# A two-layer attention trunk on one core: the first stage put in another order

## The chip, the cores and the metric

The kernel runs on one core of a Trainium2 chip. The metric is device time in microseconds (us) of one execution; three runs are given, and a profiled execution beside them. The engines: TensorE (PE, matrix products into PSUM), VectorE (DVE), ScalarE (ACT), GpSimd (POOL), and SyncE (SP), which issues most transfers.

## The reference

One sequence of 512 tokens, width 1024, two layers, each `x + rmsnorm(mixer(rmsnorm(x)))`. Layer 0 mixes by sparse attention with three branches (compressed, selected, window) in 16 heads and 4 groups, layer 1 by differential attention in 8 heads:

```python
for i in range(DEPTH):                       # 2
    u = rmsnorm(x, norm_pre[i])
    y = nsa_mixer(u, ...) if i % 2 == 0 else diff_mixer(u, ...)
    x = x + rmsnorm(y, norm_post[i])
# nsa_mixer
q, kc, vc, ks, vs, kw, vw, gate, z = split(u @ w_in)     # 1024 x 3632
o = gate0 * o_c + gate1 * o_s + gate2 * o_w              # gate = sigmoid
y = (o * silu(z)) @ w_out
# diff_mixer
q, k, v, z = split(u @ w_in)                             # 1024 x 4096
a = softmax(q1 k1 + bias) - lam * softmax(q2 k2 + bias)
y = (rmsnorm(a @ v) * (1 - lambda_init) * silu(z)) @ w_out
```

With 512 tokens all 8 selection blocks are taken, so that the selected branch is dense and causal, and the window of 512 covers the sequence.

## The kernel before

**Precision.** A projection splits each operand into a high and a low fp32r part and sums three products (high-high, low-high, high-low), line 197. Weight tiles stream from HBM: `Stream.load` (line 114) issues a transfer on SP, `Stream.split` (line 131) makes the two parts, for most tiles both on POOL (lines 165, 167); for the first two tiles the table `SP0`, `SP1` says by quarter which engine makes which (A: ACT, D: DVE, P: POOL). Each split loads the tile after next (line 170).

**Jobs.** All projections are a list of jobs, in the order in which the weights stream. `mjob` (line 190) makes 128 output columns for all tokens, 24 matmuls of 512 columns; `tjob` (line 205) makes token-major outputs, by weight tile or, with `by_token`, token by token. Each job is a generator and has a cost in ns: 5,120 for an mjob, and for a tjob by `4 * KD * 3 * n / 2.4` (line 242) with n columns: 10,240 for `vs` (n = 256), 12,160 for `vw` (n = 304). The job list begins `vs`, `vw`, then `kc0`, `kc1`, `vc0` and so on; index 2 is the first after the two.

**The pacing.** `Runner` (line 244) pulls jobs between other work. `step` runs one piece of the current job and adds its ns to the count; `upto` runs until a job is over; `spread` shares what is left up to a job among a number of slots; `knots` sets goals by head from the summed costs; `pull`, called after every score slot, runs pieces until the count is at the goal or the job limit is reached:

```python
self.done += next(self.gen)                                              # step, 255
total = sum(j.cost for j in jobs[:self.limit]) - self.done               # spread, 268
self.base, self.per = self.done, total / max(nslots, 1)                  # 269
self.ks = [(0, self.done)] + [(k, sum(j.cost for j in jobs[:index[n] + 1])) for k, n in ks]   # knots, 274
while self.i < self.limit and self.done < self.goal():                   # pull, 284
    self.step()
```

**The first stage.** SP issues the first token block (128 tokens), the two row broadcasts of the pre-norm gain (line 298, one row of 1024 values read into all 128 partitions), two weight tiles and then the other three token blocks (lines 608 to 612). `prenorm` (line 355) normalises a block: ACT squares and sums it, DVE scales it by the row's factor and the gain, PE transposes it (line 380), ACT copies the high part (`hi`, L100), DVE subtracts for the low part (`lo`, L105). Lines 665 to 668 do this for the four blocks, with 8 `run.step()` after each, and a scheduler orders the engines' work by priority. The PSUM banks are named by their use: `S` and `mm` two each, `T` three, `av` one.

**The first mixer's attention.** After the key projections and the compression (109.7 us), four groups follow (line 968). A group has eight units, `qb` in the order 3, 0, 2, 1 and both branches each, and a unit has four score slots: two score matmuls (lines 800, 801), the soft maximum (lines 792, 794), a scaling (line 850), transposes (line 856), products with V (line 870). A ninth unit, `Cmp` (its DVE product of line 918), ends the group. For groups 0 to 2 line 977 spreads four mjobs over 33 slots: `run.spread(ends[g], 33)`; before the next group `run.upto` finishes what is left. Group 3 spreads two jobs and the output projection's first part. The first half of a group is slots 1 to 16 (`qb` 3 and 0), the second half slots 17 to 32.

**The second mixer.** The second pre-norm and the value projections `dv0` to `dv3` come at about 350 to 432 us (line 1089 on; there too two jobs run as generators, and line 1100 adds their cost to the count). Then eight heads of four units with two score slots each (line 1198 on); line 1197 sets the goals of the heads' jobs, `run.upto(dends[h])` ends each head, and after the heads the output projection follows.

## Time and profile before

| | |
|---|---|
| median of 3 runs | 672.92 us (671.29 to 674.07) |
| the profiled execution | 666.73 us |
| its span, first to last instruction | 664.8 us |
| PE busy | 638.5 us (96%) |
| DVE, ACT, POOL busy | 434.2, 340.6, 402.5 us |
| first value matmul, first key projection | 11.27, 43.27 us |
| groups 0 to 3 begin | 109.7, 164.83, 220.02, 274.11 us |
| their second halves begin | 135.17, 189.46, 244.94, 293.00 us |
| the eight heads | 432 to 612 us |

PE's matmuls are pipelined: a record lasts longer than the distance from one start to the next, so a cost is read from starts, and a busy PE may still have room. "Granted clock" is the share of full speed that PE's clock had; 0.50 is 1.2 GHz, 1.00 is 2.4 GHz.

### The profile page before, as it was taken

What the parts mean: (1) busy time and instruction counts of PE and PEld (TensorE: products, weight loads), DVE (VectorE), ACT (ScalarE), POOL (GpSimd) and SP (SyncE); (2) the same over time, 40 slices, a digit from 0 to 9 for tenths busy, and PEclk for the clock granted to TensorE, in tenths of its full rate; (3) what the DMA queues carried; (4) which work ended last, traced back from release to release, by engine and by line L of the source; (5) the groups of instructions that cost most, each with busy time, mean ns of one, the idle gap of its engine ahead of it and who ended that gap; (6) DMA issues with size and microseconds to landing.
All of it is one profiled execution on the core that took longest, in us unless ns stands there. A gap on an engine that the chain in (4) does not pass through costs nothing.

```text
span 664.8 us, 11267 instructions
## 1 busy us (share of the span) xinstructions
PE 638.5 (96%) x3773; PEld 555.4 (84%) x3773; DVE 434.2 (65%) x1224; ACT 340.6 (51%) x904; POOL 402.5 (61%) x675
## 2 busy tenths in 40 slices
PE   6999999999999999999999899999999999899996
PEld 5888888888788788888887899888888887779885
DVE  4611235688878878969878700147859769996834
ACT  5311234675667567778553311235455556577531
POOL 4778568777778587758487358948465464332300
PEclk8999999999999999999999899999999999999998
DMA  7565433113022121201942222323223222114402
GB/s 251 141 166 134 124 80 93 53 34 84 12 65 65 33 63 29 53 17 48 322 149 93 96 64 76 116 65 110 65 76 84 72 72 65 64 63 155 164 26 101
DMA packets 68989, 60.52 MB, mean 91 GB/s; under 512 B 3628, under 2 KB 60868, under 8 KB 68932
## 3 DMA queue, kind: packets, MB, share of 16 engines
q1 hardware_dynamic: 68212, 57.45, 29.6%
q10 hardware_dynamic: 720, 2.36, 0.9%
q8 instruction: 30, 0.49, 0.3%
q14 instruction: 27, 0.22, 0.1%
HBM read 55.04 MB, written 4.76 MB: 90 GB/s over the span
## 4 chain that ended last, share of the span: by engine, by line
PE 74%; DVE 15%; ACT 5%; issue 3%; DMA 2%; POOL 0%; SPq 0%; DVEq 0%; ACTq 0%; POOLq 0%
PE mm L198 28%; PE mm L218 10%; PE mm L467 6%; PE T L856 5%; PE av L870 5%; PE S L218 5%; PE S L801 4%; PE S L800 3%; PE S L467 3%; DVE stk L105 3%; DVE P L792 1%; PE T L721 1%; PE av L1162 1%; DMA wraw<-in_nsa_w_in_dram 1%; ACT stk L100 1%
## 5 line engine op out<-in xcount | busy, mean ns | idle before, releaser
L167 POOL TENSOR_TENSOR wlo<-wraw,whi 128x256 fp32r<-128x256 f32 (+2 forms) x247 | 185.5, 779 | 22.9 <-DVE st L792 12.1
L165 POOL TENSOR_SCALAR whi<-wraw 128x256 fp32r<-128x256 f32 (+1 forms) x240 | 95.6, 424 | 115.0 <-PE mm L198 54.9
L794 ACT ACTIVATE P<-P,st 128x512 f32<-128x512 f32 (+3 forms) x192 | 107.4, 560 | 89.2 <-DVE st L792 88.3
L850 POOL TENSOR_SCALAR P<-P,st,gate 128x512 f32<-128x512 f32 (+3 forms) x128 | 80.1, 639 | 27.3 <-DVE st L847 22.6
L198 PE MATMUL mm<-bigA,whi 128*128 128x512 f32 x192 | 77.3, 403 | 0.1
L792 DVE CUSTOM_DVE_ANT_0 P<-S,BT 128x128 f32<-128x128 f32 (+2 forms) x144 | 59.7, 418 | 24.2 <-PE S L801 21.9
L198 PE MATMUL mm<-bigB,whi 128*128 128x512 f32 x192 | 75.4, 393 | 0.0
L198 PE MATMUL mm<-bigA,wlo 128*128 128x512 f32 x192 | 75.3, 392 | 0.0
L105 DVE TENSOR_TENSOR PT<-T,PT 128x512 fp32r<-128x512 f32 x84 | 56.9, 685 | 8.2 <-ACT PT L100 6.2
L870 PE MATMUL av<-PT,bigE 128*128 128x512 f32 x160 | 56.4, 417 | 1.1 <-DVE bigF L878 0.9
L100 ACT ACTIVATE stk<-mm 64x512 fp32r<-64x512 f32 x64 | 37.9, 591 | 33.2 <-PE mm L198 17.8
L218 PE MATMUL mm<-whi,bigF 128*128 128x256 f32 x176 | 50.4, 288 | 2.3 <-DVE stk L105 2.3
L856 PE MATMUL T<-ident,P 128*128 128x128 f32 x320 | 51.7, 272 | 0.0
L100 ACT ACTIVATE PT<-T 128x512 fp32r<-128x512 f32 x84 | 48.6, 591 | 6.1 <-PE T L856 3.9
L856 PEld LDWEIGHTS T<-ident,P 128*128 128x128 f32 x320 | 41.0, 140 | 12.3 <-issue 0.4
L198 PE MATMUL mm<-bigF,whi 128*128 128x512 f32 x128 | 51.1, 399 | 0.0
L421 DVE SCALAR_TENSOR_TENSOR stk<-mm,stk 64x512 fp32r<-64x512 f32 x32 | 22.1, 690 | 44.5 <-ACT stk L100 43.7
L198 PE MATMUL mm<-bigF,wlo 128*128 128x512 f32 x128 | 50.5, 395 | 0.0
L198 PE MATMUL mm<-bigE,whi 128*128 128x512 f32 x128 | 50.2, 392 | 0.0
L218 PE MATMUL mm<-wlo,bigF 128*128 128x256 f32 x176 | 49.9, 284 | 0.0
L218 PE MATMUL mm<-whi,bigE 128*128 128x256 f32 x176 | 49.4, 283 | 0.0
L198 PEld LDWEIGHTS mm<-bigB,whi 128*128 128x128 f32 x192 | 36.0, 188 | 8.1
(286 smaller groups left out, 1675.3 us busy)
## 6 DMA issues: line engine op xcount, KB each, us to landing
wraw<-in_diff_w_in_dram SPq DMA_DIRECT2D x31, 512.0 KB, 3.8
wraw<-in_nsa_w_in_dram SPq DMA_DIRECT2D x26, 512.0 KB, 4.0
BT<-rd SPq DMA_DIRECT2D x32, 128.0 KB, 3.2
wraw<-in_diff_w_out_dram SPq DMA_DIRECT2D x5, 512.0 KB, 3.8
bigF<-in_x_dram SPq DMA_DIRECT2D x4, 512.0 KB, 9.8
wraw<-in_nsa_w_out_dram SPq DMA_DIRECT2D x4, 512.0 KB, 3.5
bigD<-in_x_dram SPq DMA_DIRECT2D x4, 512.0 KB, 4.2
x1d<-bigD ACTq DMA_DIRECT2D x4, 512.0 KB, 5.1
```

Source lines behind the costliest of these rows:

```text
L100: return nc.scalar.activation(dst, src, AF.Copy, scale=scale)
L105: nc.vector.tensor_tensor(dst, src, h.bitcast(F32), op=OP.subtract)
L165: nc.gpsimd.tensor_scalar(h[:, a:b], v, 1.0, 0.0, op0=OP.mult, op1=OP.add)
L167: e.tensor_tensor(l[:, a:b], v, h[:, a:b].bitcast(F32), op=OP.subtract)
L198: T["mm"] = nc.tensor.matmul(p[:, a:b], wt[:, k, :], u[:, k, a:b], start=(k == 0 and j == 0), stop=(k == KD - 1 and j == 2)).ins
L218: nc.tensor.matmul(acc[t], u[:, k0 + k, t * 128:(t + 1) * 128], wt[:, k, :], start=(ci == 0 and k == 0 and j == 0 and t % per == 0), stop= ...
L467: nc.tensor.matmul(p, U[u][:, k, t * 128:(t + 1) * 128], wt[wi], start=start and j == 0, stop=stop and j == 2, skip_group_check=True)
L792: nc.vector.tensor_tensor_reduce(out=o, in0=i0, in1=b, op0=OP.add, op1=OP.min, scale=-1.0, scalar=BIG, accum_out=nm)
L794: nc.scalar.activation(pt[:, :n], pt[:, :n], AF.Exp, bias=nm, scale=-1.0, accum_out=den)
L850: NORM(nc, i, br, qb).tensor_scalar(self.P[i][:, :n], self.P[i][:, :n], st[:, 8 + i:9 + i], gate[:, NT - 1 - qb, c:c + 1], op0=OP.mult, op ...
L856: T["tmark"] = nc.tensor.transpose(p[:, j * 128:(j + 1) * 128], self.P[j][:, kb * 128:(kb + 1) * 128], ident).ins
L870: nc.tensor.matmul(av, T["V"][:, br, kb, g, :], p, start=(br == 0 and kb == 0 and j == 0), stop=(br == 1 and kb == qb and j == 1))
```

## The change

The gain row is no longer broadcast by transfers. One row goes by ACT's queue into the first partition of a zeroed tile, and two fp32 matmuls with a matrix of ones write it to all partitions of two PSUM banks. The first token block comes in two half transfers, the second one is issued ahead of the weights. The first five weight tiles are split by a table with high parts on ACT and low parts on DVE and POOL. The order of PE in the first stage is written out in `SEQ0` (s, w: one token of `vs`, `vw`; p: the transposes of a token block), `vw` goes token by token too, and the two generators are called directly; afterwards `run.i` is set to 2. The tanh of the gate is taken once at the end. `nsplit` says how many tiles a `by_token` job splits when it ends. A `by_token` job now takes one bank for each token.

```diff
-WARM = 7
+WARM = 4
...
-NS = 4
+NS = 5
...
+SEQ0 = 's0 p1 s1 w0 w1 p2 s2 w2 p3 w3 s3'.split()
-SPX = ('AP',) * 4
-SPN = 2
-SP0 = ('AP',)*4
-SP1 = ('AD','AD','PP','PP')
+SP0 = (('AP', 'AD', 'AP', 'AP'), ('AD', 'AP', 'AD', 'AP'), ('AP', 'AP', 'AD'), ('AP', 'AP', 'AD'), ('AP', 'AD'))
...
             evac(p)
         Job(name, [wcols(w, width, col, 128)], run, 24 * 512 / 2.4)
 
-    def tjob(name, w, width, col, n, evac, banks, cuts=((0, 4), (4, 4)), by_token=False):
+    def tjob(name, w, width, col, n, evac, banks, cuts=((0, 4), (4, 4)), by_token=False, nsplit=None):
         def run(i):
-            bs = [bank(b) for b in banks]
-            per = 4 // len(bs)
-            acc = [bs[t // per][:, (t % per) * n:(t % per) * n + n] for t in range(NT)]
+            if by_token:
+                per, acc = 1, [None] * NT
+            else:
+                bs = [bank(b) for b in banks]
+                per = 4 // len(bs)
+                acc = [bs[t // per][:, (t % per) * n:(t % per) * n + n] for t in range(NT)]
             cut = {}
 
             def part(ci, t):
...
                     yield 3 * n / 2.4
 
             if by_token:
                 for ci in range(len(cuts)):
                     cut[ci] = ws.cut.pop(i + ci)
                 for t in range(NT):
+                    acc[t] = bank(banks[t * len(banks) // NT])[:, :n]
                     for ci in range(len(cuts)):
                         yield from part(ci, t)
                     evac(t, acc[t])
-                for _ in cuts:
-                    if i:
-                        ws.split()
+                for _ in range(len(cuts) if nsplit is None else nsplit):
+                    ws.split()
                 return
             for ci in range(len(cuts)):
                 cut[ci] = ws.cut.pop(i + ci)
...
     def load_x(t):
         nc.sync.dma_start(xt[:, t, :], drows(x, t * 128 * D, [[D, 128], [1, D]]))
 
-    load_x(0)
-    gpre = [ptile() for _ in range(2)]
     for i in range(2):
-        nc.sync.dma_start(gpre[i], drows(npre, i * 512, [[0, 128], [1, 512]]))
+        nc.sync.dma_start(xt[:, 0, i * 512:i * 512 + 512], drows(x, i * 512, [[D, 128], [1, 512]]))
+    xn = slot("D", [128, NT, D])
+    grow = xn[:, NT - 1]
+    nc.gpsimd.memset(grow[:, 0:512], 0.0)
+    nc.vector.memset(grow[:, 512:D], 0.0)
+    T0["g"] = nc.scalar.dma_start(grow[0:1], drows(npre, 0, [[D, 1], [1, D]])).ins
+    ones = const.tile([128, 128], F32, name="ones")
+    nc.vector.memset(ones, 1.0)
     BTN = 256 + 4 * 384
     BT = [const.tile([128, BTN], F32, name=f"BT{i}") for i in range(2)]
     for t in BT:
         nc.vector.memset(t[:, 0:256], 0.0)
     ident = const.tile([128, 128], F32, name="ident")
     make_identity(nc, ident)
-    for _ in range(WARM):
-        nc.tensor.matmul(bank("T")[:, :256], BT[0][:, :128], BT[0][:, :256], start=True, stop=True)
+    def warm(n):
+        for _ in range(n):
+            nc.tensor.matmul(bank("T")[:, :256], BT[0][:, :128], BT[0][:, :256], start=True, stop=True)
+
+    warm(WARM)
+    gpre = [bank(b) for b in ("av", "mm")]
+    for i in range(2):
+        nc.tensor.matmul(gpre[i], ones, grow[:, i * 512:i * 512 + 512], start=True, stop=True)
 
     def rsqrt(y, ss, n, scale):
 
...
     def prenorm(t, src, xn, grow, uh, ul, early):
 
         halves = (slice(0, 512), slice(512, 1024))
+        whole = t and not early
         ss = [small(1, tag="ss") for _ in range(2)]
-        with tc.issue_after(T0["a"]) if "a" in T0 else ExitStack():
-            for c, s in zip(halves, ss):
+        with tc.issue_after(T0["a"]) if early and "a" in T0 else ExitStack():
+            for c, s in ((slice(0, D), ss[1]),) if whole else zip(halves, ss):
                 nc.scalar.activation(pttile(F32) if early else xn[:, c], src[:, c], AF.Square, accum_out=s)
         if early:
             for c, g in zip(halves, grow):
                 nc.gpsimd.tensor_tensor(xn[:, c], src[:, c], g, op=OP.mult)
-        m0 = part_sum(ss[0])
+        m0 = epst if whole else part_sum(ss[0])
         if early:
             r, q = row_rstd(m0, ss[1], split=True)
             for c in halves:
                 nc.vector.tensor_scalar(xn[:, c], xn[:, c], r, q, op0=OP.mult, op1=OP.mult)
         else:
             r = row_rstd(m0, ss[1])
-            for c, g in zip(halves, grow):
-                nc.vector.scalar_tensor_tensor(xn[:, c], src[:, c], r, g, op0=OP.mult, op1=OP.mult)
+            with tc.issue_after(T0["w"]) if "w" in T0 else ExitStack():
+                for c, g in zip(halves, grow):
+                    T0["s"] = nc.vector.scalar_tensor_tensor(xn[:, c], src[:, c], r, g, op0=OP.mult, op1=OP.mult).ins
 
         def turn():
             for i in range(2):
...
-                nc.scalar.activation(T["gate"][:, NT - 1 - t, :], p[:, 256:304], AF.Tanh, scale=0.5)
+                nc.scalar.activation(T["gate"][:, NT - 1 - t, :], p[:, 256:304], AF.Copy)
...
-    tjob("vs", w_in, NSA_IN, 1792, 256, evac_v(0), ("S", "S", "mm", "mm"), by_token=True)
-    tjob("vw", w_in, NSA_IN, 2304, 304, evac_v(1), ("mm", "mm", "S", "S"), cuts=((0, 3), (3, 3), (6, 2)))
+    tjob("vs", w_in, NSA_IN, 1792, 256, evac_v(0), ("S", "S", "S", "S"), by_token=True, nsplit=0)
+    tjob("vw", w_in, NSA_IN, 2304, 304, evac_v(1), ("mm", "S", "S", "mm"), cuts=((0, 3), (3, 3), (6, 2)), by_token=True,
+         nsplit=2)
...
     ws.extra.add(jobs[index['dv1']].first)
     ws.by[jobs[index['dv1']].first] = SPD
 
+    load_x(1)
     ws.load()
     ws.load()
-    load_x(1)
     load_x(2)
     load_x(3)
-
-    for _ in range(NS):
+    U["h"] = slot("A", [128, KD, S], F32R)
+    U["l"] = slot("B", [128, KD, S], F32R)
+    turns = {}
+
+    def xnorm(t):
+        turns[t] = prenorm(t, xt[:, t], xn[:, t], gpre, U["h"], U["l"], False)
+
+    xnorm(0)
+    with tc.issue_after(T0["s"]):
         ws.split()
+    with tc.manual_schedule(engines={mybir.EngineType.PE}):
+        turns[0]()
+    with tc.issue_after(T0["h"]):
+        ws.split()
+    T0["w"] = T["lo"]
+    with tc.issue_after(T0["s"]):
+        xnorm(1)
+    T0.pop("w")
 
 
     tab = const.tile([32, 16], F32, name="tab")
...
     T["V"] = slot("E", [128, 2, NT, 4, 128], F32R)
     gate = const.tile([128, NT, 48], F32, name="gate")
     T["gate"] = gate
-    U["h"] = slot("A", [128, KD, S], F32R)
-    U["l"] = slot("B", [128, KD, S], F32R)
-    xn = slot("D", [128, NT, D])
-    for t in range(NT):
-        prenorm(t, xt[:, t], xn[:, t], gpre, U["h"], U["l"], False)()
-        for _ in range(8):
-            run.step()
-
-    with tc.issue_after(T0["h"]):
-        nc.scalar.activation(small(1, tag="rstd"), epst, AF.Tanh)
+    with tc.manual_schedule(engines={mybir.EngineType.PE}):
+        gens = [jobs[index[n]].run(jobs[index[n]].first) for n in ("vs", "vw")]
+        h0 = T0["h"]
+        for w in SEQ0:
+            t = int(w[1])
+            if w[0] == "p":
+                turns[t]()
+            else:
+                for _ in range(8):
+                    next(gens["sw".index(w[0])])
+            if w == "p1":
+                with tc.issue_after(T0["h"]):
+                    for _ in range(2, NS):
+                        ws.split()
+                with tc.issue_after(T0["l"]):
+                    with tc.issue_after(h0):
+                        xnorm(2)
+                    with tc.issue_after(T0["h"]):
+                        xnorm(3)
+        for g in gens[::-1]:
+            for _ in g:
+                pass
+    run.i = 2
+    nc.scalar.activation(gate, gate, AF.Tanh, scale=0.5)
     T0.clear()
     wload = tc.issue_after(ws.last)
     wload.__enter__()
```

With the two generators called directly, the first weights of the compression (before: line 678, issued on SP right after the sixth weight tile) follow the tiles of the splits at the end of `vw`.

What the built order of PE shows elsewhere. Projection matmuls between the score matmuls of the slots, counted in it, before and after: `m` are wide ones (512 columns, L198), `d` narrow ones (256 columns, L218 before, L221 after).

| slots | before | after |
|---|---|---|
| group 0, first half / second half | m 48 / 48 | m 96 / 0 |
| group 1 | m 48 / 48 | m 96 / 0 |
| group 2 | m 48 / 48 | m 96 / 0 |
| group 3, first half | m 33 | m 48 |
| group 3, second half, to the first head | m 63, d 420 | m 48, d 420 |
| heads 0 and 1 | m 96, d 144 | m 144, d 156 |
| head 2 | m 60, d 12 | m 48 |
| head 3 | m 36, d 84 | d 36 |
| head 4 | m 54, d 12 | m 120, d 60 |
| head 5 | m 48 | m 24 |
| head 6 | m 42, d 12 | d 96 |
| head 7 | d 84 | none |

On PE, in the second half of group 1, before (`S` is a score, `T` a transposition, `av` a product with V, `mm` a projection with the weight parts `whi`, `wlo`):

```order
L800 MATMUL S_2154<-bigC_738,stk_1261 128x416
L801 MATMUL S_2154<-bigC_738,stk_1261 128x416
L198 MATMUL mm_2150<-bigA_164,whi_1959 128x512
L198 MATMUL mm_2150<-bigA_164,wlo_1960 128x512
L198 MATMUL mm_2150<-bigB_165,whi_1959 128x512
L870 MATMUL av_1934<-PT_2055,bigE_162 128x512
L800 MATMUL S_2176<-bigC_738,stk_1431 128x416
L801 MATMUL S_2176<-bigC_738,stk_1431 128x416
L198 MATMUL mm_2150<-bigA_164,whi_1959 128x512
L198 MATMUL mm_2150<-bigA_164,wlo_1960 128x512
L198 MATMUL mm_2150<-bigB_165,whi_1959 128x512
L870 MATMUL av_1934<-PT_2056,bigE_162 128x512
```

and after, at the same scores:

```order
L844 MATMUL S_2219<-bigC_734,stk_1174 128x416
L845 MATMUL S_2219<-bigC_734,stk_1174 128x416
L900 MATMUL T_2236<-ident_85,P_2133 128x128
L900 MATMUL T_2236<-ident_85,P_2147 128x128
L914 MATMUL av_1973<-PT_2125,bigE_193 128x512
L914 MATMUL av_1973<-PT_2126,bigE_193 128x512
L844 MATMUL S_2226<-bigC_734,stk_1177 128x416
L845 MATMUL S_2226<-bigC_734,stk_1177 128x416
L844 MATMUL S_2245<-bigC_734,stk_1278 128x416
L845 MATMUL S_2245<-bigC_734,stk_1278 128x416
L900 MATMUL T_2236<-ident_85,P_2173 128x128
L844 MATMUL S_2252<-bigC_734,stk_1281 128x416
```

The three projection matmuls behind each score are gone from there; score follows score, with transposes and products of earlier ones between.

On PE, in the last head (head 7), before:

```order
L218 MATMUL mm_7090<-wlo_6845,bigF_4256 128x256
L218 MATMUL mm_7090<-whi_6844,bigE_4257 128x256
L800 MATMUL S_7165<-stk_7083,stk_6959 128x128
L801 MATMUL S_7165<-stk_7084,stk_6959 128x128
L218 MATMUL mm_7090<-whi_6844,bigF_4256 128x256
L218 MATMUL mm_7090<-wlo_6845,bigF_4256 128x256
L218 MATMUL mm_7090<-whi_6844,bigE_4257 128x256
L218 MATMUL mm_7090<-whi_6844,bigF_4256 128x256
L218 MATMUL mm_7090<-wlo_6845,bigF_4256 128x256
L218 MATMUL mm_7090<-whi_6844,bigE_4257 128x256
```

and after:

```order
L844 MATMUL S_7250<-stk_6780,stk_6665 128x128
L845 MATMUL S_7250<-stk_6781,stk_6665 128x128
L844 MATMUL S_7256<-stk_6786,stk_6668 128x128
L845 MATMUL S_7256<-stk_6787,stk_6668 128x128
L844 MATMUL S_7278<-stk_6780,stk_6665 128x384
L845 MATMUL S_7278<-stk_6781,stk_6665 128x384
L844 MATMUL S_7284<-stk_6786,stk_6668 128x384
L845 MATMUL S_7284<-stk_6787,stk_6668 128x384
L1232 MATMUL T_7192<-ident_85,PT_7114 128x128
L1196 MATMUL T_7215<-ident_85,P_7175 128x128 x3
```

The narrow projection matmuls (`bigF`, `bigE` against `whi`, `wlo`) that stood behind the scores of this head are gone; four scores stand in a row.

On PE, in the first stage, at a later token's transposes (`T` from `bigD`), before:

```order
L218 MATMUL S<-whi,bigA 128x304 [waits Pool_49]
L218 MATMUL S<-wlo,bigA 128x304 [waits Pool_49]
L380 MATMUL T<-ident,bigD 128x128 [waits DVE_49,PE_49]
L380 MATMUL T<-ident,bigD 128x128 x3
L218 MATMUL mm<-bigC,bigB 128x256 [waits DVE_49]
L218 MATMUL mm<-bigC,bigA 128x256 x2
L218 MATMUL mm<-bigC,bigB 128x256
```

and after:

```order
L221 MATMUL S<-wlo,bigA 128x304
L221 MATMUL S<-whi,bigB 128x304
L397 MATMUL T<-ident,bigD 128x128 x4
L397 MATMUL T<-ident,bigD 128x128 [waits PE_49]
L397 MATMUL T<-ident,bigD 128x128 x3
L221 MATMUL S<-bigC,bigA 128x256 [waits Activation_49]
L221 MATMUL S<-bigC,bigA 128x256
L221 MATMUL S<-bigC,bigB 128x256 [waits DVE_49]
```

Before, products of another token follow the transposes. After, the products of the same token follow, and the first waits for ACT's copy and the first low part for DVE's subtraction.

## Rows read from the trace of the kernel before

**Rows 1.** The page's first lines: span, then busy time of each engine.

```profile
span 664.8 us, 11267 instructions
PE 638.5 (96%) x3773; PEld 555.4 (84%) x3773; DVE 434.2 (65%) x1224; ACT 340.6 (51%) x904; POOL 402.5 (61%) x675
```

**Rows 2.** Stretches, opening: length; busy PE, PEld, DVE, ACT, POOL; clock; DMA; GB/s.

```profile
4.00:6.00 2.00, 2.00 (x8) 1.67 (x7) 0.47 (x3) 1.63 (x5) 0.00 (x0) 1.00 0.89 181
6.50:12.00 5.50, 1.77 (x11) 1.15 (x11) 2.41 (x5) 2.60 (x8) 2.04 (x3) 0.99 1.07 395
12.00:15.20 3.20, 3.20 (x15) 3.20 (x16) 3.05 (x8) 2.76 (x9) 3.20 (x6) 0.50 0.60 180
```

**Rows 3.** Timeline of ACT: start, duration, line, operation [idle before, releaser].

```profile
9.40 1.33 ACT L100 ACTIVATE bigC<-wraw 128x256 fp32r<-128x256 f32 x4 [3.58 <-DMA wraw<-in_nsa_w_in_dram]
10.64 0.57 ACT L100 ACTIVATE bigA<-T 128x512 fp32r<-128x512 f32 x1
```

**Rows 4.** Timeline of PE, first stage, and of SyncE's queue (last row).

```profile
11.27 0.50 PE L218 MATMUL S<-bigC,bigA 128*128 128x256 f32 x2 [1.86 <-ACT bigA L100]
...
24.81 0.28 PE L218 MATMUL mm<-bigC,bigA 128*128 128x256 f32 x1
24.93 0.28 PE L218 MATMUL mm<-bigC,bigB 128*128 128x256 f32 x1
...
27.04 0.60 PE L380 MATMUL T<-ident,bigD 128*128 128x128 f32 x4
27.40 0.48 PE L218 MATMUL mm<-bigC,bigA 128*128 128x256 f32 x2
...
43.27 0.39 PE L198 MATMUL mm<-bigA,whi 128*128 128x512 f32 x1
43.50 0.39 PE L198 MATMUL mm<-bigA,wlo 128*128 128x512 f32 x1
...
27.72 0.86 SPq L678 DMA_DIRECT2D bigF<-in_nsa_cmp_w_k_dram  x1
```

**Rows 5.** Stretches: group 1's first half; groups 0-2's second halves, summed; group 3's second half.

```profile
164.83:189.46 24.63, 24.37 (x136) 19.79 (x135) 18.49 (x63) 17.37 (x46) 18.71 (x31) 1.00 0.16 43
...
sum 89.39, PE 88.50 PEld 74.62 DVE 76.82 ACT 62.31 POOL 66.43; mean PE 29.50 PEld 24.87 DVE 25.61 ACT 20.77 POOL 22.14
...
293.00:316.00 23.00, 22.19 (x152) 20.16 (x151) 20.26 (x67) 18.48 (x50) 17.19 (x25) 1.00 0.14 39
```

**Rows 6.** DVE in group 1's second half by line; line 918: least/median/most ns.

```profile
L438 DVE SCALAR_TENSOR_TENSOR zt<-zt,mm 128x512 f32<-128x512 f32 x2 | 1.4, 679 | 0.0
...
L918 DVE TENSOR_TENSOR P<-vcmp,bmask x4: 428/1818/3119, 160.8 to 320.4; 128x256 f32<-128x256 f32 x4
```

**Rows 7.** Stretches: heads 0-1; 4; 7; the others summed; all; DVE's `stk`, L438; ten us.

```profile
432.00:485.06 53.06, 51.06 (x326) 45.66 (x326) 36.25 (x93) 24.98 (x68) 30.68 (x56) 1.00 0.28 80
532.83:552.32 19.49, 19.49 (x113) 16.97 (x110) 13.47 (x44) 11.43 (x36) 11.99 (x23) 1.00 0.33 89
592.78:612.00 19.22, 17.82 (x135) 16.25 (x134) 16.16 (x44) 12.59 (x34) 1.75 (x1) 1.00 0.31 104
...
sum 107.45, PE 101.84 PEld 89.17 DVE 89.58 ACT 64.37 POOL 46.50; mean PE 20.37 PEld 17.83 DVE 17.92 ACT 12.87 POOL 9.30
...
432.00:612.00 180.00, 172.39 (x1069) 151.80 (x1068) 139.31 (x388) 100.78 (x284) 89.17 (x155) 1.00 0.26 76
...
432.00:612.00 180.00, 30.08 (x44) 1.00 0.26 76
...
432.00:612.00 180.00, 5.93 (x15) 1.00 0.26 76
...
470.00:480.00 10.00, 8.45 (x67) 7.83 (x66) 9.74 (x29) 4.90 (x13) 3.86 (x7) 1.00 0.33 95
```

**Rows 8.** Stretches around a pause of PE, columns as in rows 2.

```profile
368.00:370.00 2.00, 0.00 (x1) 0.00 (x0) 2.00 (x5) 0.42 (x3) 0.87 (x1) 1.00 1.00 362
370.00:372.00 2.00, 1.55 (x7) 1.55 (x8) 2.00 (x8) 0.40 (x2) 0.00 (x0) 0.58 0.22 88
```

More of the change, by code (lines that the diff above doesn't have):

```diff
@@ L111, in __init__ @@
             self.nload = self.ncut = 0
-            self.by = {0: SP0, 1: SP1, **{i: SPX for i in range(2, SPN)}}
+            self.by = dict(enumerate(SP0))
         def load(self):
@@ L159, in split @@
                      "P": lambda: nc.gpsimd.tensor_scalar(h[:, a:b], v, 1.0, 0.0, op0=OP.mult, op1=OP.add)}[eh]()
-                    {"D": nc.vector, "P": nc.gpsimd}[el].tensor_tensor(l[:, a:b], v, h[:, a:b].bitcast(F32), op=OP.subtract)
+                    x = {"D": nc.vector, "P": nc.gpsimd}[el].tensor_tensor(l[:, a:b], v, h[:, a:b].bitcast(F32), op=OP.subtract)
+                    if el == "D":
+                        T["lo"] = x.ins
                     continue
@@ L328, in trunk @@
     nc.vector.memset(epst, EPS)
-    nc.scalar.activation(small(1, tag="rstd"), epst, AF.Sqrt)
+    with tc.issue_after(T0["g"]):
+        nc.scalar.activation(small(1, tag="rstd"), epst, AF.Sqrt)
     def part_sum(ss, m=EPS):
```

17 lines of the change are left out of this document (7 added, 10 removed).

## The prediction

> **What bounds the kernel now.** I read the page first: TensorE (PE) is busy 638.5 of the span's 664.8 us [rows 1], so a microsecond of work or of waiting that PE is spared is a microsecond of the end, wherever PE is the last one waited for. The stretches by engine say where that holds. In the opening PE waits for data [rows 2, 3]. In the sparse-attention phase (109.7 to 316 us) the work comes in four groups of 32 score slots, with projection matmuls put between the slots as filler. The first half of such a group fills PE wholly (24.37 of 24.63 us) while VectorE (DVE) has room (18.49); in the second halves of the first three groups DVE is busy 76.82 of 89.39 us, nearly as full as PE [rows 5]. In the eight heads of the differential phase (432 to 612 us) PE is busy 172.39 of 180.00 us, DVE 139.31 [rows 7].
>
> The text of the change is about the first 43 us. The order of instructions shows a second thing, and it decides. The filler is paced by a running count, `run.done`, against a goal in nanoseconds of matmul. Before, the value projections `vs` and `vw` ran through `run.step()`, which adds their cost, 10,240 + 12,160 = 22,400 ns by the kernel's own formula. Now they run as bare generators and only `run.i` is set to 2: the count stays 22,400 behind for good, and each `spread` believes that there is that much more to do. Four filler jobs cost 20,480; the plan for 33 slots now spreads 42,880, so the real work is used up after half of them. The built order says just this: 96 and 0 filler matmuls in the two halves of a group, where 48 and 48 stood (the table under the change).
>
> **Part by part: the opening.** Removed are two row broadcasts of 256 KB each. While they were under way the core's transfers ran at 181 GB/s, and at 395 GB/s afterwards [rows 2]; 0.52 MB at 181 is 2.9 us, and the 0.52 MB of the second token block, now ahead of the first weights, is 1.3 us at 395. So the weights, whose arrival ended ScalarE's (ACT's) wait at 9.40 us [rows 3], come up to 1.6 us earlier; I take 1.2, since several transfers were in flight together. The broadcast itself becomes two fp32 matmuls on a row that lands by a small transfer: they lie beside the wait for the token block and are free unless the row lands after some 6 us (when the block itself has come, an estimate from the 9.40 of the weights behind it); then each microsecond is lost. Four warm-up matmuls instead of seven lie there too.
>
> From the first value matmul at 11.27 to the first key projection at 43.27 is 32.0 us [rows 4]. Its pure work, from the spacing of starts, is 96 matmuls of 0.12, 96 of 0.14 (the same by 304 to 256 columns) and 32 transposes at 0.36 per four: 27.8 us. The other 4.2 are waits and the stretch from 12.0 to 15.2 us, in which the granted clock was 0.50 (1.2 GHz) after PE had been busy 1.77 of 5.50 us; that costs half of 3.2, 1.6 us [rows 2]. The same work stays. It gains the missing half-clock if PE rests less, and it gains by splits on ACT and DVE in place of GpSimd (POOL). It pays for a written-out order: a token's transposes are followed at once by the matmuls that need them, where the scheduler had put others between. Two such places (tokens 2 and 3) each wait for a copy by ACT (0.57 [rows 3]) and a subtraction by DVE of the same size, about 1 us together. The third weight pair of `vw` is now needed by token 0 at once, by my estimate some 2 us before its transfer and split can be done. Sum: 5 us of waits against 4.2. Start 1.2 earlier, stretch 0.3 to 0.8 longer: I take **-1.0**, with bounds of -5 (no wait left) and +3.
>
> That upper bound holds one moved thing: on SyncE's queue the twelve transfers for the compression weights began at 27.72 us [rows 4]; they now stand behind two weight loads that wait for POOL splits at the stage's end. The matmuls that use them come after the first key projections, so I put zero.
>
> **The sparse groups.** Half a group's filler is 48 matmuls of 0.23 us (starts 43.27 and 43.50 [rows 4]): 11.0 us move from second halves to first. A first half is full, so it grows by 11.0 less what hides in small waits; I put 1 (0 to 2). A second half shrinks, but only until DVE is the bound. The three second halves hold 76.82 us of DVE, 25.6 each [rows 5]. Less the two evacuations that move along (1.4 per half [rows 6]) that is 24.2. One instruction in it, line 918, took up to 3.12 us, 1.82 at its median, for work that took 0.43 at its fastest [rows 6], while POOL ran weight splits; with the splits gone to the first half, up to 1.4 goes too: 22.8.
>
> The rows show line 918 stretched several times over. The Trainium skill (SBUF — State Buffer, "SBUF: two separate sides") gives a reason: VectorE instructions with two SBUF inputs and GpSimd share a port pair that is held for a whole instruction, and the loser waits. By that rule the second halves would be at the 22.8 end; without it at 24.2. The trace agrees in this instruction alone.
>
> How full can DVE be? In one stretch of the heads it was busy 9.74 of 10 us [rows 7], which gives 23.4 to 24.9 us a half; as full as now (76.82 of 89.39) 26.5 to 28.2. I take 25.5 against 29.8 now: -4.3. A group: 11.0 - 1 - 4.3 = +5.7 (bounds 11 - 2 - 6.4 = +2.6 and 11 - 1.6 = +9.4). Three groups: **+17** (8 to 28). The fourth has only two jobs; 15 matmuls, 3.4 us, move, and its second half (DVE 20.26 of 23.00 [rows 5]) gives back 2.2 before DVE fills 9.74 of 10: **+1.2** (0 to 3.4).
>
> **The differential heads.** Here the surplus puts whole jobs in blocks. By the table, heads 0 and 1 get 48 wide (0.23) and 12 narrow (0.12) matmuls more, 12.5 us, and head 4 gets 66 and 48 more, 20.9 us. Both stretches are PE's already (51.06 of 53.06, 19.49 of 19.49 [rows 7]), so they lengthen by 33.4, less 2. The other five heads took 107.45 us [rows 7]. Their filler falls from 65.8 to 32.4 us, so PE alone would need 74.1. DVE's share of a head without evacuations is (139.31 - 30.08 - 5.93)/8 = 12.9 us [rows 7]; filled as in the last head (16.16 of 19.22, 84%) that is 15.4 a head, 77 for five; and the 32.4 us of filler stand in blocks, beside which DVE has at most the two scores waiting in PSUM to work on. Half of it hidden gives 77 + 16 = 93, so -14.2; none hidden gives +2, all hidden with DVE fuller gives PE's 74.1, so -33. Net 31.4 - 14.2 = **+17** (-2 to +33).
>
> **The sum.** The profiled execution ran 666.73 us, 6.2 below the median of the runs, 672.92; I carry the difference over unchanged. -1.0 + 17 + 1.2 + 17 = +34.2, so 707.1, said as **707**.
>
> **Rivals.**
> A. The count's lag acts as above: 688 to 724 us. For it: the built order, and DVE's share in the second halves. Chance 0.81.
> B. Not slower. The second halves run at PE's pace without filler, as if DVE had no floor: the place is each second half, and the point is DVE work of at most 29.8 - 11.0 = 18.8 us there. Then groups and heads cost what they cost now and only the opening counts: 671.9 (668 to 676). Against it: 22.8 us is the least that the rows allow, 4 us above that point. For it: matmul records run 0.39 us where starts are 0.23 apart [rows 4], so "busy" hides room into which filler could go.
> The Trainium skill (Trainium Kernel Development and Optimization, "Performance Expectations") says as much: matmul busy time is a bad metric because matmuls are pipelined. By it alone I would put B higher; the starts, listed every 0.23 us, show little room. Chance 0.08, split between faster and same.
> C. Slower yet: unfilled stretches leave PE idle so long that the granted clock falls, as at 368 to 370 us, where PE ran nothing and the next two microseconds had 0.58 [rows 8]. PE's 18.8 us in a second half at half rate would be 37.6, 12 over the 25.5 put above; two groups so hit add 24 us: some 725 to 750. Against it: 8.45 of 10 left the clock at 1.00 [rows 7], and a score without filler waits less than a microsecond at a time. Chance 0.07.
> D. The opening does not do what it says: the gain row lands late, PE's order waits on it, and the compression weights are waited for: +4 on A, 711. Chance 0.04, inside A's range.
>
> **How the numbers follow.** The likeliest case gives 707. A and D reach 688 to 724, from the bounds taken not all at one end; that leaves out about 2 in 10 (B, C and the ends of A). 0.5% is 3.4 us, about what a measurement of this kernel can tell from no change. B gives 0.03 faster and 0.05 same; all else, 0.92, is slower.
>
> **What would show it.** In the profile after: the first key projection within 38 to 46 us; group starts some 60 us apart where they are 55; projection matmuls absent from second halves, with PE below 9 tenths and DVE above 9; in the differential phase an almost pure PE stretch of 40 us around head 4. Group starts still 55 us apart with no filler in second halves would make the floor of DVE wrong. Equal filler in both halves would make the reading of the count wrong. A granted clock below 1.00 inside groups would mean C.

## The result and the profile after

The changed kernel took 709.07 us (706.30 to 710.59), the kernel before 672.78 beside it: 1.054 of it, with an interval of 1.051 to 1.057. Forecast were 707 and a range of 688 to 724. The size came out and the cause is the one named; the runs below show that. The parts of the sum did not come out: their errors cancelled, and that the total fits so closely is luck.

The profiled execution is the fastest of the four (706.30). The head of its page, to be set beside [rows 1]:

```profile
span 704.5 us, 11264 instructions
PE 659.9 (94%) x3771; PEld 560.6 (80%) x3771; DVE 424.8 (60%) x1227; ACT 341.9 (49%) x908; POOL 390.0 (55%) x662
PEclk9999999999999999989999999999999999998999
```

PE has all but the same matmuls to do (3771 records for 3773) and is "busy" 21 us more, so this busy time is no measure of work. The weight loads are busy 555.4 [rows 1] and 560.6 us, which is 84 and 80% of the span. The Trainium skill (Trainium Kernel Development and Optimization, "Performance Expectations") calls matmul busy time a bad metric of how close a kernel is to its roofline (the most that the hardware could do), and the busy share of the weight loads a good one. This case agrees: for all but the same work the matmuls' busy time grew by 21 us and that of the weight loads by 5.

By stage, counted between score matmuls in the order in which PE runs them (first score of group 0, of group 3, of head 0, last score of head 7; 32 scores are a group, 8 a head, and the time is that of a score's second matmul):

| stage | before, us | after, us | difference | forecast |
|---|---|---|---|---|
| to the first score | 110.0 | 111.8 | +1.8 | -1.0 |
| groups 0 to 2 | 157.0 | 165.3 | +8.3 | +17 |
| group 3 to the first head | 165.3 | 181.0 | +15.8 | +1.2 |
| heads | 175.2 | 187.8 | +12.7 | +17 |
| behind them | 57.4 | 58.5 | +1.1 | 0 |
| sum | 664.8 | 704.5 | +39.7 | +34.2 |

By this count the groups begin earlier than the table of times before and [rows 5] have them: groups 1 to 3 at 158.1, 211.5 and 267.0 us, not 164.83, 220.02 and 274.11, and the second halves of groups 0 to 2 at 132.1, 186.2 and 241.7. The "second halves" of [rows 5] therefore hold work of the next group's first half. By the count they took 26.0, 25.4 and 25.4 us and not 29.8, with 22.1 us of DVE each and not 25.6.

**Groups 0 to 2.** Two stretches of the kernel before and two of the one after, each the 16 scores of a half of group 1 by that count (columns as in [rows 2]):

```profile
158.10:186.16 28.06, 27.78 (x148) 22.26 (x147) 21.08 (x63) 17.36 (x45) 21.12 (x33) 1.00 0.17 43
186.16:211.53 25.37, 25.37 (x142) 21.67 (x142) 22.07 (x75) 18.83 (x51) 18.76 (x32) 1.00 0.23 57
```

```profile
163.52:205.45 41.93, 41.93 (x223) 34.82 (x222) 27.70 (x81) 23.49 (x57) 27.00 (x45) 1.00 0.17 45
205.45:220.37 14.92, 13.99 (x74) 10.01 (x73) 14.08 (x57) 13.55 (x39) 11.77 (x21) 1.00 0.21 50
```

The first half grew by 13.9 us where 10 were forecast, and the second shrank by 10.5 where 4.3 were. DVE is busy 14.08 of 14.92 us in the second half without filler, 94%, as full as forecast; but PE is just as full (13.99 us), so DVE alone does not set its length. The half is 14.9 us long and not 25.5, because DVE's work there fell from 22.07 to 14.08 us. Where that went is told by DVE's lines. Before, second half, then first half:

```profile
L105 DVE TENSOR_TENSOR PT<-T,PT 128x512 fp32r<-128x512 f32 x13 | 8.8, 685 | 1.2 <-ACT PT L100 1.2
...
L105 DVE TENSOR_TENSOR PT<-T,PT 128x512 fp32r<-128x512 f32 x10 | 6.8, 688 | 2.7 <-ACT PT L100 2.7
```

After, second half, then first half:

```profile
L103 DVE TENSOR_TENSOR PT<-T,PT 128x512 fp32r<-128x512 f32 x5 | 3.4, 685 | 0.0
...
L103 DVE TENSOR_TENSOR PT<-T,PT 128x512 fp32r<-128x512 f32 x16 | 10.9, 688 | 4.5 <-ACT PT L98 3.8 <-PE av L914 0.6
```

Of the subtractions behind the transposes 5 are left in the second half where 13 were, and 16 stand in the first half where 10 were: they slid into the next first half, with the transposes and the products with V that PE does for them. There the filler gives DVE room. So group 1 lost 3.4 us (53.43 to 56.85) where 5.7 were forecast.

The product of line 918 (line 962 after) took up to 3.12 us before [rows 6]. By the count the products of groups 0 to 2 do not stand in the second halves: they run some 3 to 6 us into the next group's first half, before and after. After:

```profile
L962 DVE TENSOR_TENSOR P<-vcmp,bmask x4: 422/488/490, 169.0 to 342.1; 128x256 f32<-128x256 f32 x4
```

Whether one of POOL's weight splits (line 167, a subtraction of two tiles) runs beside it makes the difference. Before, once with such a split and once beside POOL's scaling of line 850:

```profile
214.77 0.74 POOL L167 TENSOR_TENSOR wlo<-wraw,whi 128x256 fp32r<-128x256 f32 x1
...
214.99 3.12 DVE L918 TENSOR_TENSOR P<-vcmp,bmask 128x256 f32<-128x256 f32 x1
...
269.20 1.34 POOL L850 TENSOR_SCALAR P<-P,st,gate 128x256 f32<-128x256 f32 x2
269.77 0.43 DVE L918 TENSOR_TENSOR P<-vcmp,bmask 128x256 f32<-128x256 f32 x1
```

Before, it took 1.49 to 3.12 us beside line 167 and 0.43 beside the scaling alone; after, with no split at its place, 0.49 at most. The Trainium skill (SBUF — State Buffer, "SBUF: two separate sides") says that a VectorE instruction with two SBUF inputs and a GpSimd instruction share a port pair, which one of them holds for its whole length. The traces agree with it beside the splits; beside the scaling no such wait is seen.

**Group 3.** Before, the first 8 scores, the next 8, and from the 25th score to the end of the group's last unit:

```profile
267.02:283.83 16.81, 16.81 (x95) 13.96 (x93) 15.31 (x40) 12.57 (x29) 13.30 (x20) 1.00 0.16 43
283.83:292.15 8.32, 8.32 (x54) 7.18 (x54) 5.11 (x26) 5.52 (x20) 6.40 (x13) 1.00 0.02 2
303.01:328.40 25.39, 24.54 (x178) 22.13 (x177) 22.67 (x58) 17.42 (x43) 18.01 (x24) 1.00 0.55 180
```

and the same stretches after:

```profile
277.13:301.29 24.16, 24.16 (x129) 19.88 (x128) 18.73 (x50) 15.03 (x34) 13.78 (x20) 1.00 0.10 25
301.29:313.40 12.11, 8.39 (x41) 6.61 (x40) 9.85 (x33) 8.66 (x25) 9.38 (x15) 0.76 0.15 43
322.24:353.30 31.06, 27.93 (x181) 24.06 (x180) 18.55 (x53) 14.96 (x37) 12.08 (x19) 0.95 0.61 200
```

The first 8 scores take 27 of the wide matmuls more (42 for 15, counted in the trace), 6.2 us at 0.23, and grow by 7.4. The next 8 have 12 fewer (6 for 18) and should shrink by 2.8; they grow by 3.8. The third 8 have none for 15 and shrink by 2.0. PE is busy 8.39 of 12.11 us in the second 8, the granted clock is 0.76, and DVE has six subtractions for the output projection's operand in it that stood later before, around its 25th score. DVE's work on the tile `bigB` in that stretch, before and then after (length, busy):

```profile
283.83:292.15 8.32, 0.00 (x0) 1.00 0.02 2
```

```profile
301.29:313.40 12.11, 5.34 (x6) 0.76 0.15 43
```

PE's waits there, from its list of waits (us in total, times, longest):

```profile
PE S L844 <- DVE st L836: 3.7, 3, 1.7
```

The 0.76 is a stretch at the full clock and one at half of it:

```profile
301.29:307.40 6.11, 4.14 (x28) 3.45 (x27) 4.33 (x16) 5.09 (x13) 5.53 (x9) 1.00 0.00 0
307.60:313.40 5.80, 4.05 (x14) 2.96 (x14) 5.32 (x18) 3.36 (x13) 3.65 (x7) 0.50 0.32 90
```

The last stretch has the same 103 matmuls of the output projection in both and is 5.7 us longer, with the clock at 0.95.

**Heads.** Stretches of the kernel after: head 3, head 4, head 7 (from first score to first score, the last to the last score).

```profile
539.03:549.16 10.13, 9.02 (x64) 7.83 (x62) 9.46 (x32) 10.00 (x35) 2.84 (x5) 1.00 0.35 93
549.16:596.84 47.68, 44.59 (x255) 38.40 (x253) 30.47 (x76) 17.46 (x48) 26.59 (x50) 1.00 0.24 70
632.87:646.01 13.14, 8.70 (x45) 7.24 (x44) 11.66 (x45) 8.30 (x30) 0.94 (x1) 0.74 0.47 177
```

Before, these three took 26.26, 20.61 and 12.51 us. Head 4 has the block of 47.7 us; head 3 without wide filler is done in 10.1, with DVE and ACT at 9.46 and 10.00. Head 7, which gave up all its filler, is longer than before: PE busy 8.70 of 13.14 us at a clock of 0.74.

**The clock.** Over the whole span the granted clock was 0.982 after and 0.992 before. Length times the missing share is the most that it can cost, 12.7 and 5.3 us: an estimate of at most 7 of the 39.7 us.

### The profile page after: what moved, and what is told of

It reads as the page before. It is cut to its first block, busy times and chain, and to the rows that moved or that the text cites. A ratio compares the mean times of both kernels' runs of the same rounds, so it can differ in the third digit from the quotient of the medians.

```text
span 704.5 us, 11264 instructions
## 1 busy us (share of the span) xinstructions
PE 659.9 (94%) x3771; PEld 560.6 (80%) x3771; DVE 424.8 (60%) x1227; ACT 341.9 (49%) x908; POOL 390.0 (55%) x662
## 4 chain that ended last, share of the span: by engine, by line
PE 70%; DVE 15%; ACT 6%; issue 6%; POOL 2%; DMA 1%; DVEq 0%; SPq 0%; ACTq 0%; POOLq 0%
PE mm L198 29%; PE mm L221 7%; PE mm L481 6%; PE S L221 5%; PE av L914 4%; PE T L900 4%; PE S L481 3%; PE S L844 3%; PE S L845 3%; DVE P L836 2%; DVE stk L103 1%; PE av L1206 1%; ACT stk L98 1%; PE T L765 1%; ACT P L838 1%
## 5 line engine op out<-in xcount | busy, mean ns | idle before, releaser
L167 POOL TENSOR_TENSOR wlo<-wraw,whi 128x256 fp32r<-128x256 f32 (+1 forms) x239 | 177.5, 770 | 38.5 <-ACT whi L163 38.3
L165 POOL TENSOR_SCALAR whi<-wraw 128x256 fp32r<-128x256 f32 x232 | 91.5, 420 | 123.5 <-PE mm L198 61.7
L894 POOL TENSOR_SCALAR P<-P,st,gate 128x512 f32<-128x512 f32 (+3 forms) x128 | 77.4, 616 | 39.4 <-DVE st L891 21.4
L198 PE MATMUL mm<-bigA,whi 128*128 128x512 f32 x192 | 76.7, 400 | 0.1
L198 PE MATMUL mm<-bigB,whi 128*128 128x512 f32 x192 | 76.1, 396 | 0.0
L198 PE MATMUL mm<-bigA,wlo 128*128 128x512 f32 x192 | 75.5, 393 | 0.0
L914 PE MATMUL av<-PT,bigE 128*128 128x512 f32 x160 | 62.4, 437 | 1.3 <-DVE PT L103 0.8
L900 PE MATMUL T<-ident,P 128*128 128x128 f32 x320 | 54.0, 276 | 2.4 <-POOL P L894 1.8
L198 PE MATMUL mm<-bigF,whi 128*128 128x512 f32 x128 | 51.0, 398 | 3.7 <-DVE stk L103 3.2
L435 DVE SCALAR_TENSOR_TENSOR stk<-mm,stk 64x512 fp32r<-64x512 f32 x32 | 22.1, 690 | 51.4 <-ACT stk L98 50.9
L221 PE MATMUL mm<-whi,bigF 128*128 128x256 f32 x176 | 50.0, 286 | 2.0 <-DVE stk L103 1.7
L198 PE MATMUL mm<-bigF,wlo 128*128 128x512 f32 x128 | 50.0, 391 | 0.0
L198 PE MATMUL mm<-bigE,whi 128*128 128x512 f32 x128 | 50.0, 390 | 0.0
L221 PE MATMUL mm<-wlo,bigF 128*128 128x256 f32 x176 | 49.7, 283 | 0.0
L221 PE MATMUL mm<-whi,bigE 128*128 128x256 f32 x176 | 49.4, 283 | 0.0
L198 PEld LDWEIGHTS mm<-bigB,whi 128*128 128x128 f32 x192 | 36.1, 188 | 7.6
```

What stands on the lines that cost most here:

```text
L165: nc.gpsimd.tensor_scalar(h[:, a:b], v, 1.0, 0.0, op0=OP.mult, op1=OP.add)
L167: e.tensor_tensor(l[:, a:b], v, h[:, a:b].bitcast(F32), op=OP.subtract)
L198: T["mm"] = nc.tensor.matmul(p[:, a:b], wt[:, k, :], u[:, k, a:b], start=(k == 0 and j == 0), stop=(k == KD - 1 and j == 2)).ins
L221: T["tm"] = nc.tensor.matmul(acc[t], u[:, k0 + k, t * 128:(t + 1) * 128], wt[:, k, :], start=(ci == 0 and k == 0 and j == 0 and t % per == 0),
L894: NORM(nc, i, br, qb).tensor_scalar(self.P[i][:, :n], self.P[i][:, :n], st[:, 8 + i:9 + i], gate[:, NT - 1 - qb, c:c + 1], op0=OP.mult, op ...
L900: T["tmark"] = nc.tensor.transpose(p[:, j * 128:(j + 1) * 128], self.P[j][:, kb * 128:(kb + 1) * 128], ident).ins
```

## The experiments

Theory P: the count that lags by 22,400 makes the loss, by the filler's place. Rival O: the rebuilt first stage itself.

**Count put right in the changed kernel**

```diff
     run.i = 2
+    run.done += jobs[index["vs"]].cost + jobs[index["vw"]].cost
```

> The changed kernel with the two value projections' cost added to the count behind `run.i = 2`; nothing else. Theory P (the count's lag makes the loss): the filler stands as before, 48 and 48 in a group, so only the rebuilt first stage is left, which in the two traces brings group 0's first score from 110.01 to 111.84 us: 672.8 + 1.8 = 674.6, 672 to 677. Rival O (the rebuilt first stage itself upsets what follows, by the banks, queues or splits that it leaves behind): about 709 still.

674.52 us, 1.0076 of before (1.0038 to 1.0114). The filler counted in the built order is that of before again, and 4.6 of the 5.4% are gone. O falls. What is left, 0.4 to 1.1%, is what the rebuilt first stage can cost.

**The lag alone, in the kernel before**

```diff
+    run.done -= jobs[index["vs"]].cost + jobs[index["vw"]].cost
     with tc.issue_after(T0["h"]):
         nc.scalar.activation(small(1, tag="rstd"), epst, AF.Tanh)
```

> The kernel before with 22,400 taken off the count behind the first stage; nothing else. P: filler as in the changed kernel, first stage as before: 709.1 - 1.8 = 707.3, 704 to 711. O: 672.8, as before.

706.61 us, 1.057 of before (1.053 to 1.061). The lag without any of the rebuilt stage makes the whole loss. This and the run before it are the two sides of the proof. They do not add up to the last per cent (5.7 and 0.8 for 5.4 together), and the record does not show why.

**The lag taken away in one phase**

```diff
+    run.done += ...              # behind run.i = 2 (groups); at group 3's spread (fourth); ahead of run.knots (heads)
...
+    run.done -= ...              # at group 3's spread (groups); behind run.upto("oA") (fourth)
```

> The changed kernel with the count put right for groups 0 to 2 only (the 22,400 are taken off again where group 3 begins). From the two traces, first score to first score, groups 0 to 2 lost 3.6 + 3.4 + 1.3 = 8.3 us: 709.1 - 8.3 = 700.8, 698 to 704. By the prediction's own term for them (17) it would be 692.

> The changed kernel with the count put right only where the heads' goals are set. From the traces, first score of head 0 to last score of head 7, the heads lost 187.84 - 175.17 = 12.7 us: 709.1 - 12.7 = 696.4, 693 to 700. By the prediction's term for them (17): 692. If the heads' loss were not the pacing: 709.

> The changed kernel with the count put right for group 3 alone (from its start to the end of its part of the output projection). By the traces, from its first score to the end of its last unit, group 3 lost 15.3 us: 709.1 - 15.3 = 693.8, 690 to 698. By the prediction's term for it (1.2): 708.

700.65, 700.48 and 695.32 us: 1.048 (1.044 to 1.052), 1.048 (1.044 to 1.052) and 1.038 (1.035 to 1.041). The forecasts started from 709.1, which was measured beside a before of 672.8; beside these runs before took 669.7. So the ratios count, and not how near 700.65 and 695.32 lie to 700.8 and 693.8. By them the three give back 0.6, 0.6 and 1.6% of before, or 4, 4 and 11 us, where the traces said 8.3, 12.7 and 15.3: all three fall short, and the heads miss their bounds in microseconds too (700.48, bounds 693 to 700). The prediction's terms for groups and group 3 are refuted either way (1.2 us for group 3 would be a ratio of 1.052, 17 for the groups 1.029). Together it is 2.8%, less than the 4.6% of the whole correction.

The profiles show where the rest went. Each phase that was put right, in its own run:

```profile
113.42:269.22 155.80, 154.44 (x849) 129.62 (x848) 123.76 (x402) 108.27 (x284) 117.17 (x198) 1.00 0.21 52
...
463.57:642.20 178.63, 170.50 (x1029) 149.96 (x1028) 135.43 (x378) 97.58 (x275) 88.84 (x155) 0.98 0.24 69
...
277.94:446.84 168.90, 163.20 (x1074) 147.48 (x1073) 101.09 (x269) 79.07 (x205) 114.02 (x172) 0.98 0.31 99
```

Against the changed kernel's 165.3, 187.8 and 181.0 these are 9.5, 9.2 and 12.1 us less, 30.8 together, and 4.6% is 31 us. So each phase gives its share back at its own place, and much of what is missing in the total was lost elsewhere in the same executions: the first score came at 113.4, 115.3 and 112.5 us for 111.8, and the heads took 190.9 us for 187.8 in the run with the groups put right.

**Which of group 3's two plans**

```diff
+            run.done -= ...       # count_fourth, but already ahead of run.spread("oA", ...)
             run.spread("oA", 33 - 4 * ZN - ODELAY)
```

> The changed kernel with the count put right for the first of group 3's two plans alone (the two projections up to `z7`), and lagging again for the second (the output projection's first part). The run with both put right was 695.3. If group 3's loss is the missing wide filler behind its 17th score: 695, 692 to 698. If it is the output projection's matmuls drawn forward (72 for 57 in the last 16 slots): 705 to 709.

695.51 us, as with both plans right (695.32). The output projection's matmuls drawn forward cost nothing that these runs can tell; the wide ones of the first plan, drawn into the first 8 scores and missing behind them, cost it.

**Half the lag**

```diff
+    run.done -= 11200
```

> The kernel before with half the lag (11,200) taken off the count. Filler in groups 0 to 2 is 69 and 27 (48 and 48 without lag, 96 and 0 with the whole), group 3 as with the whole lag (48 wide ones in its first half, none in its second). If a half loses only where PE has less to do than DVE, the 27 matmuls left (6.2 us) cover DVE in groups 0 to 2, which lose 0 to 2 us instead of 8.3; group 3 loses its 12 to 15; the heads, with blocks of half the size, 4 to 8: 669.7 + 21 = 690, 686 to 695. If the loss is in proportion to what is moved: 669.7 + 37 / 2 = 688 with 4 us of it in groups 0 to 2.

682.93 us, 1.018 of before (1.016 to 1.021): a third of the whole lag's loss, less than either reading gave. By the traces the groups 0 to 2 took 161.5 us (157.0 before, 165.2 with the whole lag), so they lost in proportion, and the cover that was expected of 27 matmuls (the trace has 24) is wrong; from group 3 to the first head it was 172.9 (165.3, 180.3), in the heads 181.5 (175.2, 190.3). The profile of this run in its second half of group 1:

```profile
195.86:214.82 18.96, 18.05 (x97) 14.49 (x97) 15.49 (x58) 13.96 (x39) 16.57 (x30) 1.00 0.23 62
```

PE is busy 18.05 of 18.96 us there and DVE 15.49: DVE does not fill it, and yet the group is longer.

**A lead instead of a lag**

```diff
     run.done += jobs[index["vs"]].cost + jobs[index["vw"]].cost
+    run.done += 5120
```

(on the kernel with the scheduler's PE order, below)

> The run with the scheduler's PE order and the right count (669.1), with one job's cost (5,120) too much in the count: filler is drawn later, 36 and 60 in a group for 48 and 48, and the heads get theirs later too. If the plan without lag or lead is already the one in which neither half waits, 1 to 4 us slower; if the first halves have more room than the second halves, faster by up to 2.

698.47 us, 1.041 of before (1.039 to 1.043). The miss is large: one job too much in the count costs 29 us beside 669.13 without it. The groups don't mind (156.6 us for 155.8), the heads do. The eight heads, and what follows them, with the lead and then without:

```profile
435.87:631.91 196.04, 178.92 (x985) 152.12 (x984) 133.15 (x378) 97.32 (x273) 86.99 (x154) 0.91 0.24 69
631.91:696.42 64.51, 56.31 (x318) 48.72 (x316) 34.51 (x92) 23.49 (x66) 10.34 (x7) 0.99 0.26 94
```

```profile
431.16:609.80 178.64, 170.51 (x1029) 149.87 (x1027) 135.47 (x378) 97.69 (x275) 88.73 (x155) 0.98 0.24 69
609.80:667.62 57.82, 51.23 (x274) 43.44 (x272) 33.71 (x93) 22.38 (x64) 8.59 (x6) 0.99 0.34 127
```

17 us in the heads at a clock of 0.91, 7 behind them. PE's longest waits in the heads tell what for, with the lead and then without:

```profile
PE S L846 <- ACT stk L98: 8.4, 10, 1.5
PE S L847 <- DVE stk L103: 4.5, 10, 0.8
```

```profile
PE S L846 <- DVE stk L103: 3.1, 4, 1.3
PE mm L221 <- DVE stk L103: 2.3, 3, 1.0
```

`stk` is an operand of the scores, made from wide projections. With the lead each of the eight heads has 48 of them by the trace, where 60, 36, 60, 36, 54, 48, 42 and none stood: they come late, and the scores wait for their own operand. The clock can have cost at most 14 of the 17 us (196.04 us at 0.91, 178.64 at 0.98); how much is the wait alone is not shown. The plan without lag or lead is the best of those that were tried.

**The first stage: transposes earlier, and the scheduler's order**

```diff
-SEQ0 = 's0 p1 s1 w0 w1 p2 s2 w2 p3 w3 s3'.split()
+SEQ0 = 's0 p1 s1 w0 p2 w1 s2 p3 w2 s3 w3'.split()
...
-    with tc.manual_schedule(engines={mybir.EngineType.PE}):
+    with ExitStack():                                        # pe_free, with SEQ0 as it was
         gens = [jobs[index[n]].run(jobs[index[n]].first) for n in ("vs", "vw")]
```

> The changed kernel with the count put right, and in `SEQ0` the transposes of tokens 2 and 3 one product block earlier (p2 between w0 and w1, p3 between s2 and w2). If the stage's loss is the waits for the copies behind the transposes (0.25 us before the first product and some 0.5 before the first low part, at two places), 1 to 2 us come back: 0.997 to 0.9985 of the run with the count put right. If the tokens' own norms are late there, no change or longer.

> The changed kernel with the count put right, and the first stage's PE order left to the scheduler in place of `SEQ0`. If the written-out order is what makes the stage longer (34.0 us from first value matmul to first key projection, against 32.0 before), 2 to 4 us come back, to about the time before; if it is the loads or the splits, nothing changes.

Transposes earlier: 674.38 us, 1.0073 (1.0042 to 1.0104), no change against 1.0076. The scheduler's order: 669.13 us, 0.998 of before (0.996 to 0.9996), and the fastest of all runs. From the first value matmul to the first key projection, with the written-out order and then with the scheduler's (count right in both):

```profile
9.74:43.99 34.25, 30.31 (x216) 28.01 (x217) 18.07 (x41) 15.13 (x38) 11.56 (x21) 1.00 0.28 81
```

```profile
11.01:41.66 30.65, 29.17 (x216) 27.87 (x217) 18.19 (x41) 13.34 (x36) 11.58 (x20) 1.00 0.30 85
```

Same work, both at full clock, 3.6 us apart. PE's waits in that stretch, written-out order:

```profile
PE S L221 <- ACT bigA L98: 1.3, 3, 0.8
PE mm L221 <- ACT whi L98: 1.2, 1, 1.2
PE S L221 <- DVE bigB L103: 1.0, 3, 0.5
PE mm L221 <- POOL wlo L158: 0.5, 1, 0.5
```

With the scheduler's order the waits for `whi` and `wlo`, the weight parts of `vw`, are not in the list. So the written-out order is what the stage loses by, and 1.7 of the 3.6 us are `vw` for token 0 set ahead of its weights, which the prediction named and priced. The other 1.9 us are not placed. That the transposes have no part in them is not shown: with them earlier the time stayed, but that profile's stretch took 33.15 us at a clock of 0.95.

**The gain row by transfers again**

```diff
-    T0["g"] = nc.scalar.dma_start(grow[0:1], drows(npre, 0, [[D, 1], [1, D]])).ins
+    gpre = [ptile() for _ in range(2)]
+    for i in range(2):
+        T0["g"] = nc.sync.dma_start(gpre[i], drows(npre, i * 512, [[0, 128], [1, 512]])).ins
...
-    gpre = [bank(b) for b in ("av", "mm")]
-    for i in range(2):
-        nc.tensor.matmul(gpre[i], ones, grow[:, i * 512:i * 512 + 512], start=True, stop=True)
```

(on the kernel with the scheduler's order)

> The run with the scheduler's PE order and the right count (669.1), with the gain row broadcast by two transfers again in place of the two fp32 matmuls. If the matmul broadcast is worth its place, the first value matmul comes 1 to 2 us later and the time is 0.2 to 0.3% longer than that run; if the weights and token blocks set the start anyway, the same.

673.00 us, 1.003 of before (1.002 to 1.004), against 0.998 with the matmuls. ACT's square of the second token block with the transfers, and with the matmuls:

```profile
10.05 1.06 ACT L376 ACTIVATE bigD<-bigF 128x1024 f32<-128x1024 f32 x1 [4.92 <-DMA bigF<-in_x_dram]
```

```profile
7.70 1.06 ACT L377 ACTIVATE bigD<-bigF 128x1024 f32<-128x1024 f32 x1 [2.32 <-DMA bigF<-in_x_dram]
```

The block lands 2.3 us earlier without the broadcasts, and the first value matmul starts at 11.01 instead of 12.22 us. This part of the change is a gain.

**The kernel before once more**

> The kernel before, unchanged, for its profile on this chip: PE's half-rate stretches in it tell whether those of the runs with the count put right (530.8 to 534.2 and 582.0 to 585.4 us, in the heads) belong to the change. If they belong to the chip, this profile has one or two there as well, of 3.4 us each; if to the change, it has only those in the opening and at 370 us.

671.78 us. Ten microseconds in the heads, this execution and then the profiled one of before:

```profile
576.00:586.00 10.00, 8.26 (x37) 6.60 (x36) 7.92 (x20) 5.14 (x13) 1.89 (x3) 0.83 0.18 52
```

```profile
576.00:586.00 10.00, 10.00 (x56) 8.48 (x55) 8.84 (x22) 7.33 (x23) 4.16 (x8) 1.00 0.12 46
```

A stretch at half the clock is there in one execution of the same kernel and not in the other. So those in the heads of the runs with the count put right need not belong to the change. The first score of this execution comes at 112.7 us, 2.7 later than in the profiled one of before: a stage of one profile is known to some 2 or 3 us only.

## Why the prediction was right, and where it was not

- **The reading of the count** held: by putting it right (1.0076) and by the lag alone (1.057).
- **The opening**, -1.0 with bounds of -5 and +3: 0.4 to 1.1% of before, 2.5 to 7.6 us, by the run with the count right; +1.8 in the trace. The step that failed is "5 us of waits against 4.2": the start came 0.7 us earlier (10.58 us for the 11.27 of [rows 4]), but the stretch to the first key projection was 34.0 us for 32.0, although the half clock of [rows 2] was not in it. The stretch holds 24 transposes and not 32, so its pure work is 27.1 us: 4.9 us of waits before, and 6.9 after. The wait for `vw`'s weights at token 0 was named, with "some 2 us", and took 1.7 with the count put right. Which profile is taken matters here: the first score comes at 111.8 and 111.3 us with the rebuilt stage, at 110.0 and 112.7 without, so the traces do not place the loss; the runs with the written-out and with the scheduler's order (1.0076 and 0.998 of before) do.
- **The groups**, +17: 8.3. DVE filled to 94%, within the 0.86 to 0.97 that was assumed, but PE did as well, against the "PE below 9 tenths" of the signs. The step that failed is the DVE work of a half, "22.8 us is the least that the rows allow": it was 14.1. Some 3.5 us of that are the stretches of [rows 5], which begin too late and so count DVE work of the next group (25.6 for 22.1). Most of the rest is that the subtractions behind the transposes slid into the next first half. The 1.4 us of line 918 was priced in a half in which that product does not run. Work that follows PE's order goes where PE's order puts it; it is no constant of a stretch.
- **Group 3**, +1.2: 15.8 to the first head, and 695.32 with that phase put right. Two failures: the first half was counted as one, 33 and 48, where 27 matmuls more crowd its first 8 scores and 12 are missing from the next 8; and a stretch that loses its filler was taken to give back, where the next 8 scores took 3.8 us longer and the third 8 gave back only 2.0. Some of the time is shown (six subtractions of another job, 5.34 us, in the way of the scores; a clock of 0.76 and 0.95), some is not: of the 5.7 us of the last stretch, a clock of 0.95 over 31.06 us explains some 1.6.
- **The heads**, +17: 12.7. The mechanism and the place (the block at head 4) held. Head 4 grew by 27 us where 20.9 were said, heads 0 and 1 by 10 where 12.5 were, and the others gave back 24 where 14 were.
- **Rival B** was half right: second halves did shrink to 14.9 us, with PE and DVE both full and DVE's work below B's point of 18.8, but the time came back in the first halves. **Rival C** is there in part, though not in groups 0 to 2: a clock of 0.76 after the filler ends in group 3, 0.74 in the last head, at most some 7 us in all, for which the sum had no term. What was held against it, that a score without filler waits less than a microsecond at a time, did not hold: PE waited up to 1.7 us at a time in group 3.
- **The sum** came out by luck: the groups were priced 9 us too high and the heads 4, group 3 15 too low and the opening 3.

## What to carry to other kernels

A hand-written order that goes round a planner must hand the planner everything that the planner's own path would have kept, its running cost as well as its position: one missing line cost 4.6% here, hundreds of microseconds behind the edit. Count the built order by stretches before and after a change, count it as finely as the stretches that you price, and let the count of scores set where a stretch begins and ends. Filler matmuls are worth their place only beside an engine that has something else to do, and they are themselves work that something waits for: too early (a lag of 22,400) cost 5 to 6%, too late (a lead of 5,120) 4%. The Trainium skill (Perfetto Trace Analysis, "Optimization Strategy") says that interleaving stretches with different bounds may improve a kernel; what the runs add is what it costs when the places are missed.
